# Moving the silu, product and split of an expert's hidden values behind TensorE's part of them, and parking the second embedding's products in DRAM

## The chip, the cores and the metric

One core of one Trainium2 chip runs the whole program. The metric is device time in microseconds (us), from one execution of the program, median of several; lower is better. The engines are TensorE (PE, with its weight loads shown apart as PEld), VectorE (DVE), ScalarE (ACT), GpSimd (POOL) and SyncE (SP), whose queue (SPq) issues nearly all the loads of weights.

## The reference

A trunk of two layers over 256 tokens of width 1024, all in float32. Nearly all of the change lies in the second layer's mixture of experts: each token goes to 2 of 8 experts, and each expert is a SwiGLU of width 3584. After it a per-layer embedding is added, which multiplies a product `p @ w_proj` (1024 columns for 256 tokens) by a gate.

```python
def swiglu_of_expert(xb, e):
    g, u = jnp.split(xb @ w_gate_up[e], 2, axis=-1)   # 1024 -> 2 x 3584
    return (jax.nn.silu(g) * u) @ w_down[e]           # 3584 -> 1024
...
h = h + moe_swiglu(rmsnorm(h, norm_ffn_g[i]), moe_router[j], moe_w_gate_up[j], moe_w_down[j])
h = h + per_layer_embed(h, p[i], norm_ple_g[i], ple_w_proj[i], ple_w_gate[i])
def per_layer_embed(h, p_i, g_norm, w_proj, w_gate):
    gate = jax.nn.sigmoid(rmsnorm(h, g_norm) @ w_gate)
    return (p_i @ w_proj) * gate
```

## The kernel before

Layer 0 and layer 1's mixers take about the first 520 us; layer 1's experts take most of the rest, to about 1450 us; the embedding's gate and the last norm follow.

**Weights.** An expert's weights come in tiles of 1 MB ("raw" tiles, `r_gu` for gate and up, `r_d` for down, `r_dl` for the last ones), loaded by SP into 11 buffers. Float32 products are made of two parts of the weights: `wsplit` writes for each half tile a high part `h` or `h_d` (a copy with rounding on ACT, line 145) and a low part `l` or `l_d` (raw minus high, on DVE, line 146). Both go through 4 buffers each.

**Experts.** The program goes through the experts 0 to 7 in order of their load, the most loaded first. Experts 0 to 3 ("large") have 128 slots and three products for each tile (high by high, low by high, high by low). Experts 4 to 7 ("few") have 64 slots; the high and low part of the tokens lie side by side in the 128 columns, so that two products do for each tile.

**Chunks.** The 3584 channels of an expert are cut into chunks of 1024, 1024, 1024 and 512. `gate_up(e, c)` multiplies a chunk's gate and up weights over 8 channel tiles k of the input, into banks `mg` and `mu`. Meanwhile the chunk before is finished: at the first row of tile k = 1 (`MID`), the function `mid()` calls `h_T`, which makes of the chunk before what `down` multiplies with the down weights. `down` then runs after the products of `gate_up`; `between` calls `activate`, which empties `mg` and `mu`, in the middle of it.

**Hidden values.** A block is 512 channels, so a chunk has two blocks, and the last has one. For a large expert `activate` makes silu and product (lines 1191 and 1192), and `h_T` transposes a block on PE (`mt`, line 1220) and splits it into `mhh` and `mhl`. For a few expert `activate` only copies gate and up out (`msg`, `msu`, line 1188), and `h_T` does for each block: 16 small products by `both` on PE that turn the block and add its two halves (`mt`, in one of 2 banks), the silu on ACT (`mgu`, line 1211), the product on DVE (`mgu`, line 1212), and the split, `mh` on ACT (line 197) and on DVE (line 198). These 16 products are called a turn below.

**Order.** Nothing of this is the final order: a scheduler puts the instructions of each engine in a fixed order by its own costs, and each engine then works its list from the top. An instruction that waits holds back all that stand behind it on that engine.

**The embedding's products.** The four tiles `pj` (128 by 512) of the second embedding are made early: `todo` holds those that are left for `mid()` of chunk 1 of expert 0 (`LATE`), and ACT copies them out (line 387). They stay in 4 of the 12 buffers of the tag `s2`, which also holds `msg`, `msu`, `mgu`, `mh`, `mhh` and `mhl`, until the end.

Of the kernel before, what the change touches and what calls it, by code (L numbers as in the profile page):

```python
# [8 lines left out]
F32 = mybir.dt.float32  # L9
F32R = mybir.dt.float32r  # L10
I32 = mybir.dt.int32
AF = mybir.ActivationFunctionType
ALU = mybir.AluOpType
AX = mybir.AxisListType
MUL, ADD, SUB, MAX = ALU.mult, ALU.add, ALU.subtract, ALU.max

P = 128
D = 1024
T = 256
NB = 2  # L20
# [4 lines left out]
NE = 8  # L25
# [58 lines left out]
def trunk_kernel(  # L84
# [6 lines left out]
    pe, act, dve, pool, sync = nc.tensor, nc.scalar, nc.vector, nc.gpsimd, nc.sync  # L91
# [5 lines left out]
    dr = ctx.enter_context(tc.tile_pool(name="dr", bufs=1, space=bass.MemoryType.DRAM))  # L97
# [5 lines left out]
    def s2(name, shape, dt=F32):  # L103
        return ar.tile(list(shape), dt, tag="s2", name=name, bufs=S2_BUFS)

    def py(name, shape=(P, 512)):
        return ps.tile(list(shape), F32, tag="y", name=name, bufs=2)

    def pt(name, shape=(P, 512)):
        return ps.tile(list(shape), F32, tag="t", name=name, bufs=2)  # L110
# [41 lines left out]
    def after(*names):  # L152

        stack = ExitStack()
        for n in names:
            stack.enter_context(tc.issue_after(last[n].ins))
        return stack
# [15 lines left out]
    def mm(o, a, b, start, stop, shared=False):  # L173
        last["mm"] = pe.matmul(o, a, b, start=start, stop=stop, skip_group_check=shared)  # L174
# [20 lines left out]
    def split(dst, src, scale=None):  # L195
        if scale is None:
            last["high"] = act.copy(dst[0], src)
            last["split"] = dve.tensor_tensor(dst[1], src, dst[0].bitcast(F32), SUB)
        else:
            last["high"] = act.activation(dst[0], src, AF.Copy, scale=scale)  # L200
            last["split"] = dve.scalar_tensor_tensor(dst[1], src, scale, dst[0].bitcast(F32), MUL, SUB)

    def sub2(pr, *idx):
        return pr[0][idx], pr[1][idx]
# [738 lines left out]
    def layer1_moe(pT):  # L943
# [110 lines left out]
        def few(e):  # L1054
            return e >= FEW
# [106 lines left out]
        def products(e, triples, start, stop):  # L1162


            if not few(e):
                return mm3s(triples, start, stop)
            for part in range(2):
                for o, a, b in triples:
                    mm(o, a, b[part], start and part == 0, stop and part == 1)

        def gate_up(e, c, mid):
            ns = CHUNKS[c][1] // 512
            banks = [[pa(f"m{nm}{e}{c}{i}") for i in range(ns)] for nm in "gu"]
            for k, j, wt in gate_up_weights(e, c):
                if (k, j) == (MID, 0):
                    mid()
                products(e, [(banks[j][i], tokens[e][k], sub2(wt, slice(None), slice(i * 512, i * 512 + 512))) for i in range(ns)],
                         k == 0, k == KT - 1)

            def activate():  # L1180

                res = []
                with after("wcopy", "wsplit"):
                    for i in range(ns):
                        if few(e):
                            res.append([s2(f"ms{nm}{e}{c}{i}", [P, 512]) for nm in "gu"])
                            for j in range(2):
                                act.copy(res[i][j], banks[j][i])
                            continue
                        sg = s2(f"msg{e}{c}{i}", [P, 512])  # L1190
                        act.activation(sg, banks[0][i], AF.Silu)
                        dve.tensor_tensor(sg, banks[1][i], sg, MUL)
                        res.append(sg)
                return res

            return activate

        def h_T(e, c, sgs):

            res = []  # L1200

            for i, sg in enumerate(sgs):
                if few(e):

                    q = pt(f"mt{e}{c}{i}", (P, 2, 4, P // 2))
                    for j in range(2):
                        for g in range(2):
                            for k in range(2):
                                mm(q[:, j, 2 * g + k, :], sg[j][:, 256 * g + k : 256 * g + 256 : 2], both, True, True)
                    t = s2(f"mgu{e}{c}{i}", [P, 4, P // 2])  # L1210
                    act.activation(t, q[:, 0], AF.Silu)
                    dve.tensor_tensor(t, q[:, 1], t, MUL)
                    hT = s2(f"mh{e}{c}{i}", [P, 4, 2, P // 2], F32R)
                    split((hT[:, :, 0], hT[:, :, 1]), t)
                    res += [hT[:, k].rearrange("q i s -> q (i s)") for k in range(4)]
                    continue
                q = pt(f"mt{e}{c}{i}", (P, 4, P))
                for g in range(2):
                    for k in range(2):
                        pe.transpose(q[:, 2 * g + k, :], sg[:, 256 * g + k : 256 * g + 256 : 2], ident)  # L1220
                hT = (s2(f"mhh{e}{c}{i}", [P, 4, P], F32R), s2(f"mhl{e}{c}{i}", [P, 4, P], F32R))
                split(hT, q)
                res += [sub2(hT, slice(None), k) for k in range(4)]
            return res

        def down(e, c, hT, yb, between):

            c0, n = CHUNKS[c]
            res = None
            for g in range(n // 256):  # L1230
                nm = f"d{e}_{c}_{g}"
                view = expert(moe_w_down, e)[c0 + g * 256 : c0 + g * 256 + 256].rearrange("(q k) c -> q k c", k=2)
                wt = wload(view, (2, D), nm, spare(nm))
                for i in range(2):
                    products(e, [(yb[half], hT[2 * g + i], sub2(wt[i], slice(None), HALF[half])) for half in range(2)],
                             c == g == i == 0, c == len(CHUNKS) - 1 and g == n // 256 - 1 and i == 1)
                if g == n // 512 - 1 and between:
                    res = between()
            return res

        def combine(e, yb, half):
            s = slice(half * 512, half * 512 + 512)
# [5 lines left out]
                mm(q, slots[e][:, b, :], yp[1], False, True)  # L1248
                dve.scalar_tensor_tensor(h[:, b, s], q, Gr[:, b, e : e + 1], h[:, b, s], MUL, ADD)

        yb, hT = {}, {}
        both = sm("both", (P, P // 2))
        dve.tensor_tensor(both, ident[:, : P // 2], ident[:, P // 2 :], ADD)

        def back(e, c, between=None):
            if c == 0:
                yb[e] = [py(f"y{e}{half}") for half in range(2)]
            if (e, c) == (NE - 1, len(CHUNKS) - 1):
                part = hT.pop((e, c))
                rows = expert(moe_w_down, e)[CHUNKS[c][0] :].rearrange("(g q k) c -> g q k c", k=2, q=P)  # L1260
                for half in range(2):
                    raw = wr.tile([P, 4, 512], F32, tag="raw", name=f"r_dl{half}", bufs=RAW_BUFS)
                    for g in range(2):
                        sync.dma_start(raw[:, 2 * g : 2 * g + 2], rows[g][:, :, HALF[half]])
                    wt = wsplit(raw, f"dl{half}")
                    for k in range(4):
                        products(e, [(yb[e][half], part[k], wt[k])], False, k == 3)
                    combine(e, yb[e], half)
                    last_norm[1](half)
                return  # L1270
            res = down(e, c, hT.pop((e, c)), yb[e], between)
            if c == len(CHUNKS) - 1:
                for half in range(2):
                    combine(e, yb[e], half)
            return res

        def more_slots(e, pos):

# [58 lines left out]

            return over > P, more

        prev = None  # L1340
        for e in range(NE):
            for c in range(len(CHUNKS)):
                if e % 2 == 1 and c == 2 and e <= FEW - 1:
                    spread_slots = gather(e // 2 + 1)
                if (e, c) == (FEW, 1):
                    spread_slots()

                def mid():
                    if prev:
                        hT[prev] = h_T(*prev, sg)  # L1350
                    if (e, c) == (0, LATE):
                        for bn in todo:
                            product(*bn, pt)
                            copy(*bn)

                activate = gate_up(e, c, mid)
                if prev:
                    sg = back(*prev, activate)
                else:
                    sg = activate()  # L1360
                    with after("wsplit"):
                        gates()
                prev = e, c
        mid()
        last_norm = halves_norm_T("ple1")
        back(*prev)

        return pj1, (last_norm[0], last_norm[2]()), overflow

# [79 lines left out]
RAW_BUFS = 11  # L1449
PAD = 8  # L1450
CONV_DVE = (31, 31, 5, 9)
MID = 1
FEW = 4
X_DVE = (3, 7)
PRODUCTS = (0, 2, 1, 0)
LATE = 1
# [36 lines left out]
```

## Time and profile before

| | |
|---|---|
| median of 3 runs | 1497.31 us (1495.36 to 1500.3) |
| the profiled execution | 1497.28 us |
| its span in the profile | 1495.5 us |
| mean granted TensorE clock | 0.995 of full speed |
| busy, share of the span | PE 97%, DVE 85%, ACT 72%, POOL 0% |
| moved by DMA | 438.26 MB |

The span is the time from the first to the last recorded instruction. Busy shares are averages over parts with different limits, so each part is read by itself: large experts until about 1010 us, few experts from about 1040 to 1446 us, then the tail.

### The profile page before, as it was taken

The numbers are of one execution on the slowest core, as the hardware profiler recorded it, in microseconds if no ns is written. First come the engines' busy times: TensorE is split into PE (matmuls) and PEld (weight loads), VectorE is DVE, ScalarE is ACT, GpSimd is POOL, SyncE is SP. The second block draws the span as 40 slices with busy tenths as digits, with TensorE's granted clock in tenths as the row PEclk, the third lists the DMA queues.
The fourth block names the chain that finished last, engine by engine and source line by source line (L and its number), as shares of the span: only waits on it lengthen the run. The fifth ranks groups of instructions, "written<-read, shape, count | busy, mean of one in ns | idle before, by whom it ended". The sixth has DMA issues, their size and how long they took to land.

```text
span 1495.5 us, 22012 instructions
## 1 busy us (share of the span) xinstructions
PE 1444.5 (97%) x7726; PEld 1194.7 (80%) x7726; DVE 1268.0 (85%) x1716; ACT 1076.1 (72%) x1441; POOL 4.9 (0%) x14
## 2 busy tenths in 40 slices
PE   7999999999999999999999999999999999999996
PEld 6999899988888878888888888886766666666665
DVE  6778655556698699999999989989999999999997
ACT  6545544446547678887887877779988988988975
POOL 0000000000000000000000000000000000000000
PEclk9999999999999999999999999999999999999998
DMA  9614656555452469898898998999999999999961
GB/s 350 241 43 131 216 177 196 172 195 185 147 203 106 149 248 354 327 410 333 322 376 336 392 347 341 359 363 389 377 409 414 390 413 410 388 413 408 394 254 44
DMA packets 136610, 438.26 MB, mean 293 GB/s; under 512 B 9067, under 2 KB 34188, under 8 KB 122412
## 3 DMA queue, kind: packets, MB, share of 16 engines
q1 hardware_dynamic: 132960, 433.19, 77.3%
q10 hardware_dynamic: 3148, 2.31, 0.5%
q0 software_dynamic: 384, 1.29, 0.4%
q8 instruction: 62, 1.02, 0.3%
q14 instruction: 56, 0.46, 0.1%
HBM read 434.92 MB, written 1.84 MB: 292 GB/s over the span
## 4 chain that ended last, share of the span: by engine, by line
PE 71%; DVE 18%; issue 4%; ACT 4%; DMA 3%; ACTq 0%; DVEq 0%; POOL 0%; POOLq 0%
PE y L174 14%; PE mg L174 11%; PE mu L174 11%; DVE l L146 11%; PE fu L174 4%; PE fg L174 4%; PE fd L174 4%; PE wo L174 3%; PE pg L174 3%; PE mt L174 2%; DMA r_gu<-in_moe_w_gate_up_dram 2%; DVE l_d L146 2%; PE p L174 1%; PE mt L1220 1%; PE in_og L174 1%
## 5 line engine op out<-in xcount | busy, mean ns | idle before, releaser
L146 DVE TENSOR_TENSOR l<-r_gu,h 128x1024 fp32r<-128x1024 f32 x448 | 526.3, 1218 | 18.1 <-ACT h L145 6.3
L145 ACT CAST h<-r_gu 128x1024 fp32r<-128x1024 f32 x448 | 456.6, 1052 | 60.2 <-PE mu L174 22.4
L146 DVE TENSOR_TENSOR l_d<-r_d,h_d 128x1024 fp32r<-128x1024 f32 x220 | 258.6, 1219 | 16.7 <-ACT h_d L145 10.4
L145 ACT CAST h_d<-r_d 128x1024 fp32r<-128x1024 f32 x220 | 226.8, 1054 | 24.7 <-PE mu L174 10.3
L146 DVE TENSOR_TENSOR l_gu<-r_gu,h_gu 128x1024 fp32r<-128x1024 f32 x44 | 53.8, 1224 | 47.7 <-ACT h_gu L145 47.7
L145 ACT CAST h_gu<-r_gu 128x1024 fp32r<-128x1024 f32 x44 | 46.0, 1048 | 64.2 <-PE fu L174 49.0
L174 PE MATMUL y<-l_d,mh 128*128 128x512 f32 x216 | 75.3, 430 | 3.7 <-DVE l_d L146 3.7
L174 PE MATMUL y<-l_d,mhh 128*128 128x512 f32 x224 | 69.8, 393 | 0.1
L174 PE MATMUL y<-h_d,mh 128*128 128x512 f32 x216 | 69.2, 402 | 0.3
L174 PE MATMUL y<-h_d,mhh 128*128 128x512 f32 x224 | 69.4, 391 | 0.0
L174 PE MATMUL y<-h_d,mhl 128*128 128x512 f32 x224 | 69.1, 390 | 0.0
L174 PEld LDWEIGHTS y<-l_d,mh 128*128 128x128 f32 x216 | 34.4, 188 | 27.4 <-DVE l_d L146 25.1
L146 DVE TENSOR_TENSOR l_fd<-r_fd,h_fd 128x1024 fp32r<-128x1024 f32 x22 | 26.9, 1224 | 27.3 <-ACT h_fd L145 26.3
L174 PE MATMUL fg<-x_ffn0h,h_gu 128*128 128x256 f32 x176 | 49.9, 283 | 0.0
L174 PE MATMUL fu<-x_ffn0h,h_gu 128*128 128x256 f32 x176 | 49.9, 283 | 0.0
L174 PE MATMUL fg<-x_ffn0h,l_gu 128*128 128x256 f32 x176 | 49.9, 283 | 0.0
L174 PE MATMUL fu<-x_ffn0l,h_gu 128*128 128x256 f32 x176 | 49.8, 283 | 0.0
L174 PE MATMUL fu<-x_ffn0h,l_gu 128*128 128x256 f32 x176 | 49.8, 283 | 0.0
L174 PE MATMUL fg<-x_ffn0l,h_gu 128*128 128x256 f32 x176 | 49.8, 283 | 0.0
L174 PEld LDWEIGHTS y<-h_d,mhl 128*128 128x128 f32 x224 | 42.1, 188 | 8.9
L174 PEld LDWEIGHTS y<-l_d,mhh 128*128 128x128 f32 x224 | 41.5, 188 | 9.5 <-DVE l_d L146 1.4
L174 PEld LDWEIGHTS y<-h_d,mhh 128*128 128x128 f32 x224 | 41.8, 188 | 8.9 <-ACT h_d L145 0.4
(719 smaller groups left out, 3673.6 us busy)
## 6 DMA issues: line engine op xcount, KB each, us to landing
r_gu<-in_moe_w_gate_up_dram SPq DMA_DIRECT2D x192, 1024.0 KB, 7.7
r_d<-in_moe_w_down_dram SPq DMA_DIRECT2D x110, 1024.0 KB, 7.7
r_gu<-in_moe_w_gate_up_dram SPq DMA_DIRECT2D x64, 512.0 KB, 6.4
r_gu<-in_ffn_w_gate_up_dram SPq DMA_DIRECT2D x44, 512.0 KB, 4.4
r_fd<-in_ffn_w_down_dram SPq DMA_DIRECT2D x11, 1024.0 KB, 4.9
r_wo<-in_ev_w_out_dram SPq DMA_DIRECT2D x4, 1024.0 KB, 12.8
r_pg<-in_ple_w_gate_dram SPq DMA_DIRECT2D x4, 1024.0 KB, 7.0
r_wo<-in_od_w_out_dram SPq DMA_DIRECT2D x4, 1024.0 KB, 5.0
```

Source lines behind the costliest of these rows:

```text
L145: last["wcopy"] = act.copy(wh, raw[:, i : i + step])
L146: last["wsplit"] = dve.tensor_tensor(wl, raw[:, i : i + step], wh.bitcast(F32), SUB)
L174: last["mm"] = pe.matmul(o, a, b, start=start, stop=stop, skip_group_check=shared)
L1220: pe.transpose(q[:, 2 * g + k, :], sg[:, 256 * g + k : 256 * g + 256 : 2], ident)
```

## The change

The part of `h_T` that belongs to a few expert is taken apart. Where all of it was called at k = 1, four functions are now called at the channel tiles `MIDS` = (1, 3, 2, 5) of the next `gate_up`: `turn` (PE) at k = 1, `turned` (silu on ACT and product on DVE, of both blocks, into one tile `mgu`) at k = 3, `across` (the large experts' transposes) at k = 2 and the split `h_T` at k = 5. The loop over `back` goes by blocks instead of chunks. The four `pj` tiles are written to a DRAM tile `pj1d` by ACT's queue, right after they are made, and loaded again by SP's queue ahead of the last block; in between their `s2` buffers serve the hidden values.

```diff
-        def gate_up(e, c, mid):
+        def gate_up(e, c, at):
 ...
-                if (k, j) == (MID, 0):
-                    mid()
+                if j == 0 and k in at:
+                    at[k]()
...
-        def h_T(e, c, sgs):
+        def turn(e, c):
             res = []
-            for i, sg in enumerate(sgs):
-                if few(e):
-                    q = pt(f"mt{e}{c}{i}", (P, 2, 4, P // 2))
-                    for j in range(2):
-                        for g in range(2):
-                            for k in range(2):
-                                mm(q[:, j, 2 * g + k, :], sg[j][:, 256 * g + k : 256 * g + 256 : 2], both, True, True)
-                    t = s2(f"mgu{e}{c}{i}", [P, 4, P // 2])
-                    act.activation(t, q[:, 0], AF.Silu)
-                    dve.tensor_tensor(t, q[:, 1], t, MUL)
-                    hT = s2(f"mh{e}{c}{i}", [P, 4, 2, P // 2], F32R)
-                    split((hT[:, :, 0], hT[:, :, 1]), t)
-                    res += [hT[:, k].rearrange("q i s -> q (i s)") for k in range(4)]
-                    continue
...
+            for i, sg in enumerate(hidden[e, c]):
+                q = pt(f"mt{e}{c}{i}", (P, 2, 4, P // 2))
+                for j in range(2):
+                    for g in range(2):
+                        for k in range(2):
+                            mm(q[:, j, 2 * g + k, :], sg[j][:, 256 * g + k : 256 * g + 256 : 2], both, True, True)
+                res.append(q)
             return res
...
+        def turned(e, c, banks):
+            t = s2(f"mgu{e}{c}", [P, len(banks), 4, P // 2])
+            for i, q in enumerate(banks):
+                act.activation(t[:, i], q[:, 0], AF.Silu)
+                dve.tensor_tensor(t[:, i], q[:, 1], t[:, i], MUL)
+            hidden[e, c] = t
+
+        def across(e, c, i):
+            if few(e):
+                return None
+            q = pt(f"mt{e}{c}{i}", (P, 4, P))
+            for g in range(2):
+                for k in range(2):
+                    pe.transpose(q[:, 2 * g + k, :], hidden[e, c][i][:, 256 * g + k : 256 * g + 256 : 2], ident)
+            return q
+
+        def h_T(e, c, i, q):
+            if few(e):
+                hT = s2(f"mh{e}{c}{i}", [P, 4, 2, P // 2], F32R)
+                split((hT[:, :, 0], hT[:, :, 1]), hidden[e, c][:, i])
+                return [hT[:, k].rearrange("q i s -> q (i s)") for k in range(4)]
...
+        stored = dr.tile([P, NB, 2, 512], F32, name="pj1d")
...
+            def turn_fresh():
+                if fresh and few(fresh[0]):
+                    banks["fresh"] = turn(*fresh)
+                if now == (0, LATE):
+                    for bn in todo:
+                        product(*bn, pt)
+                        copy(*bn)
+                    for b, i in BLOCKS:
+                        act.dma_start(stored[:, b, i], pj1[b][i])
+
+            def fresh_turned():
+                if "fresh" in banks:
+                    turned(*fresh, banks["fresh"])
...
+                activate = gate_up(*now, dict(zip(MIDS, (turn_fresh, fresh_turned, blocks_across, blocks_split))))
...
         last_norm = halves_norm_T("ple1")
-        back(*prev)
+        for b, i in BLOCKS:
+            pj1[b][i] = s2(f"pj1{b}{i}", [P, 512])
+            sync.dma_start(pj1[b][i], stored[:, b, i])
+        hT[downs[0]] = h_T(*downs[0], across(*downs[0]))
+        back(*downs[0])
...
-MID = 1
+MIDS = (1, 3, 2, 5)
```

What the scheduler makes of it is read from the built programs. The first place is on ACT, where expert 4's chunk 1 is turned while the down weights of its chunk 0 are split (names `h_d_x_2` and `h_d_x_3` are the high parts of that chunk's third and fourth raw tile, whose numbers go from 0). Before:

```order
L145 CAST h_d_0_2_0_11315<-r_d_0_2_11313 128x1024
L145 CAST h_d_0_2_1_11319<-r_d_0_2_11313 128x1024
L1211 ACTIVATE mgu_11390<-mt_11381 128x256
L145 CAST h_d_0_3_0_11333<-r_d_0_3_11331 128x1024
L145 CAST h_d_0_3_1_11337<-r_d_0_3_11331 128x1024
L197 CAST mh_11393<-mgu_11390 128x4x64
L1211 ACTIVATE mgu_11405<-mt_11396 128x256
```

and after:

```order
L145 CAST h_d_0_2_0_11316<-r_d_0_2_11314 128x1024
L145 CAST h_d_0_2_1_11320<-r_d_0_2_11314 128x1024
L1215 ACTIVATE mgu_11436<-mt_11382 128x256
L1215 ACTIVATE mgu_11436<-mt_11391 128x256
L145 CAST h_d_0_3_0_11334<-r_d_0_3_11332 128x1024
L145 CAST h_d_0_3_1_11338<-r_d_0_3_11332 128x1024
L197 CAST mh_11477<-mgu_11436 128x4x64
```

The silu of the second block has moved from behind the fourth raw tile's high parts to ahead of them. The same two lists stand at 8 places, the turns of chunks 1 and 2 of the experts 4 to 7. On DVE at the same place, before:

```order
L146 TENSOR_TENSOR l_d_0_2_1_11320<-r_d_0_2_11313,h_d_0_2_1_11319 128x1024
L1212 TENSOR_TENSOR mgu_11390<-mt_11381,mgu_11390 128x256
L146 TENSOR_TENSOR l_d_0_3_0_11334<-r_d_0_3_11331,h_d_0_3_0_11333 128x1024
L146 TENSOR_TENSOR l_d_0_3_1_11338<-r_d_0_3_11331,h_d_0_3_1_11337 128x1024
L198 TENSOR_TENSOR mh_11393<-mgu_11390,mh_11393 128x4x64
```

and after:

```order
L146 TENSOR_TENSOR l_d_0_2_1_11321<-r_d_0_2_11314,h_d_0_2_1_11320 128x1024
L1216 TENSOR_TENSOR mgu_11436<-mt_11382,mgu_11436 128x256
L146 TENSOR_TENSOR l_d_0_3_0_11335<-r_d_0_3_11332,h_d_0_3_0_11334 128x1024
L146 TENSOR_TENSOR l_d_0_3_1_11339<-r_d_0_3_11332,h_d_0_3_1_11338 128x1024
L1216 TENSOR_TENSOR mgu_11436<-mt_11391,mgu_11436 128x256
```

Here the first product and the low parts behind it stand where they stood; the second product comes ahead of the split. PE's list is the same in both at these places. The third place is ACT at the turn of chunk 0, in the middle of `gate_up` of chunk 1 (experts 5 to 7 alike; expert 4 has its own order). Before:

```order
L145 CAST h_1_3_1_11183<-r_gu_1_3_11177 128x1024
L1211 ACTIVATE mgu_11130<-mt_11121 128x256
L145 CAST h_1_4_0_11197<-r_gu_1_4_11195 128x1024
L197 CAST mh_11133<-mgu_11130 128x4x64
L1211 ACTIVATE mgu_11145<-mt_11136 128x256
L145 CAST h_1_4_1_11201<-r_gu_1_4_11195 128x1024
```

and after:

```order
L145 CAST h_1_3_1_11173<-r_gu_1_3_11167 128x1024
L1215 ACTIVATE mgu_11177<-mt_11123 128x256
L1215 ACTIVATE mgu_11177<-mt_11132 128x256
L145 CAST h_1_4_0_11192<-r_gu_1_4_11190 128x1024
L145 CAST h_1_4_1_11196<-r_gu_1_4_11190 128x1024
L197 CAST mh_11218<-mgu_11177 128x4x64
```

Both silus now stand ahead of `h_1_4_0`. On DVE the two products here stand behind `l_1_3_0` and `l_1_3_1`, ahead of `l_1_4_0`. The single-block turns of chunk 3 stand as before.

## Rows read from the trace of the kernel before

**Rows 1.** The page's first part: span, and busy time of each engine.

```profile
span 1495.5 us, 22012 instructions
PE 1444.5 (97%) x7726; PEld 1194.7 (80%) x7726; DVE 1268.0 (85%) x1716; ACT 1076.1 (72%) x1441; POOL 4.9 (0%) x14
```

**Rows 2.** Windows, large then few: busy us, engine by engine, PEclk, DMA share, GB/s.

```profile
560.00:1010.00 450.00, 449.85 (x2058) 373.20 (x2057) 416.05 (x407) 353.85 (x384) 0.00 (x0) 1.00 0.94 355
1040.00:1446.00 406.00, 388.23 (x1730) 277.61 (x1729) 389.31 (x389) 353.76 (x430) 0.00 (x0) 1.00 1.01 400
```

**Rows 3.** DVE's groups, 1040 to 1446: busy us, mean ns, idle before, releaser.

```profile
L146 DVE TENSOR_TENSOR l<-r_gu,h 128x1024 fp32r<-128x1024 f32 x206 | 238.0, 1216 | 0.1
L146 DVE TENSOR_TENSOR l_d<-r_d,h_d 128x1024 fp32r<-128x1024 f32 x106 | 122.8, 1217 | 8.2 <-ACT h_d L145 8.2
L1212 DVE TENSOR_TENSOR mgu<-mt,mgu 128x256 f32<-128x256 f32 x27 | 11.4, 421 | 7.8 <-ACT mgu L1211 7.7
```

**Rows 4.** The waits of all engines, 1040 to 1446: us in total, times, longest.

```profile
PEld mu L174 <- DVE l L146: 42.8, 74, 0.8
ACT mgu L1211 <- PE mt L174: 32.7, 18, 3.4
ACT h L145 <- DMA r_gu<-in_moe_w_gate_up_dram: 0.9, 2, 0.6
```

**Rows 5.** The waits of SP's queue, 1050 to 1440, the largest.

```profile
SPq L766 <- DVE l L146: 94.1, 52, 4.2
```

**Rows 6.** Timeline of expert 5's chunk 1 turn: start, us, [idle before <-releaser].

```profile
1175.62 1.11 PE L174 MATMUL mt<-both,msu 128*128 128x64 f32 x8
1176.77 0.38 ACT L1211 ACTIVATE mgu<-mt 128x256 f32<-128x256 f32 x1 [2.01 <-PE mt L174]
1177.05 1.98 ACT L145 CAST h_d<-r_d 128x1024 fp32r<-128x1024 f32 x2
1177.18 0.42 DVE L1212 TENSOR_TENSOR mgu<-mt,mgu 128x256 f32<-128x256 f32 x1 [0.59 <-ACT mgu L1211]
1177.96 1.11 PE L174 MATMUL mt<-both,msu 128*128 128x64 f32 x8
1178.12 2.36 DVE L146 TENSOR_TENSOR l_d<-r_d,h_d 128x1024 fp32r<-128x1024 f32 x2 [0.51 <-ACT h_d L145]
```

**Rows 7.** Timeline: the first (expert 4) and the last (expert 7) such turn pairs.

```profile
1066.50 1.11 PE L174 MATMUL mt<-both,msu 128*128 128x64 f32 x8
1068.83 1.11 PE L174 MATMUL mt<-both,msu 128*128 128x64 f32 x8
...
1423.71 1.11 PE L174 MATMUL mt<-both,msu 128*128 128x64 f32 x8
1426.05 1.11 PE L174 MATMUL mt<-both,msu 128*128 128x64 f32 x8
```

**Rows 8.** Timeline of expert 5's chunk 0 turn, in the middle of chunk 1.

```profile
1157.34 2.35 DVE L146 TENSOR_TENSOR l<-r_gu,h 128x1024 fp32r<-128x1024 f32 x2
1158.47 0.39 ACT L1211 ACTIVATE mgu<-mt 128x256 f32<-128x256 f32 x1 [0.26 <-PE mt L174]
1158.75 1.04 ACT L145 CAST h<-r_gu 128x1024 fp32r<-128x1024 f32 x1
1160.28 1.22 DVE L146 TENSOR_TENSOR l<-r_gu,h 128x1024 fp32r<-128x1024 f32 x1
```

**Rows 9.** Timeline of PE at expert 0's first products.

```profile
531.11 0.50 PE L174 MATMUL mg<-h,xe0h 128*128 128x512 f32 x1 [0.75 <-ACT pj L387]
```

**Rows 10.** The last raw tiles, by tile and by timeline: issue, landing, first use.

```profile
L145 ACT CAST h_dl<-r_dl x4: 1046/1047/1052, 1448.6 to 1451.4; 128x1024 fp32r<-128x1024 f32 x4
DMA to landing us min/median/max: 8.4/9.0/9.6
...
1422.45 3.56 SPq L1264 DMA_DIRECT2D r_dl<-in_moe_w_down_dram  x4
```

**Rows 11.** A DMA issue on ACT's queue: ns min/median/max, first and last start.

```profile
L798 ACTq DMA_DIRECT2D bd<-fbs x4: 326/344/448, 394.4 to 409.2; - x4
```

More of the change, by code (lines that the diff above doesn't have):

```diff
@@ L1196, in gate_up @@
             return activate
-        def h_T(e, c, sgs):
+        def turn(e, c):
             res = []
-            for i, sg in enumerate(sgs):
-                if few(e):
-                    q = pt(f"mt{e}{c}{i}", (P, 2, 4, P // 2))
-                    for j in range(2):
-                        for g in range(2):
-                            for k in range(2):
-                                mm(q[:, j, 2 * g + k, :], sg[j][:, 256 * g + k : 256 * g + 256 : 2], both, True, True)
-                    t = s2(f"mgu{e}{c}{i}", [P, 4, P // 2])
-                    act.activation(t, q[:, 0], AF.Silu)
-                    dve.tensor_tensor(t, q[:, 1], t, MUL)
-                    hT = s2(f"mh{e}{c}{i}", [P, 4, 2, P // 2], F32R)
-                    split((hT[:, :, 0], hT[:, :, 1]), t)
-                    res += [hT[:, k].rearrange("q i s -> q (i s)") for k in range(4)]
-                    continue
[L1217 to L1223, printed above, removed]
-            return res
@@ L1226, in down @@
-        def down(e, c, hT, yb, between):
+            for i, sg in enumerate(hidden[e, c]):
[5 more added lines that the diff above has]
+                res.append(q)
+            return res
+        def turned(e, c, banks):
[4 more added lines that the diff above has]
+            hidden[e, c] = t
@@ new lines, in across @@
+        def across(e, c, i):
[11 more added lines that the diff above has]
+                return [hT[:, k].rearrange("q i s -> q (i s)") for k in range(4)]
+            hT = (s2(f"mhh{e}{c}{i}", [P, 4, P], F32R), s2(f"mhl{e}{c}{i}", [P, 4, P], F32R))
+            split(hT, q)
+            return [sub2(hT, slice(None), k) for k in range(4)]
@@ L1228, in down @@
+        def down(e, c, i, hT, yb, between):
             c0, n = CHUNKS[c]
-            res = None
-            for g in range(n // 256):
+            for g in range(2 * i, 2 * i + 2):
                 nm = f"d{e}_{c}_{g}"
@@ L1233, in down @@
                 wt = wload(view, (2, D), nm, spare(nm))
[L1234 to L1239, printed above, removed]
+                for k in range(2):
+                    products(e, [(yb[half], hT[2 * (g % 2) + k], sub2(wt[k], slice(None), HALF[half])) for half in range(2)],
+                             c == g == k == 0, c == len(CHUNKS) - 1 and g == n // 256 - 1 and k == 1)
+                if g == 2 * i and between:
+                    between()
         def combine(e, yb, half):
@@ L1249, in combine, with back @@
                 dve.scalar_tensor_tensor(h[:, b, s], q, Gr[:, b, e : e + 1], h[:, b, s], MUL, ADD)
-        yb, hT = {}, {}
+        yb, hT, hidden = {}, {}, {}
         both = sm("both", (P, P // 2))
         dve.tensor_tensor(both, ident[:, : P // 2], ident[:, P // 2 :], ADD)
-        def back(e, c, between=None):
-            if c == 0:
+        def back(e, c, i, between=None):
+            if c == i == 0:
                 yb[e] = [py(f"y{e}{half}") for half in range(2)]
+            part = hT.pop((e, c, i))
             if (e, c) == (NE - 1, len(CHUNKS) - 1):
-                part = hT.pop((e, c))
                 rows = expert(moe_w_down, e)[CHUNKS[c][0] :].rearrange("(g q k) c -> g q k c", k=2, q=P)
@@ L1270, in back @@
                 return
-            res = down(e, c, hT.pop((e, c)), yb[e], between)
+            down(e, c, i, part, yb[e], between)
             if c == len(CHUNKS) - 1:
@@ L1274, in back @@
                     combine(e, yb[e], half)
-            return res
         def more_slots(e, pos):
@@ L1338, in overflow @@
             return over > P, more
[L1340 to L1363, printed above, removed]
@@ L1364, in layer1_moe, with blocks_across, blocks_split, between @@
-        mid()
-        last_norm = halves_norm_T("ple1")
-        back(*prev)
+        gates_up = [(e, c) for e in ORDER for c in range(len(CHUNKS))]
+        downs = [(e, c, n) for e in ORDER for c in range(len(CHUNKS)) for n in range(CHUNKS[c][1] // 512)]
+        stored = dr.tile([P, NB, 2, 512], F32, name="pj1d")
+        fresh = None
+        while gates_up or len(downs) > 1:
+            now = gates_up.pop(0) if gates_up else None
+            step = NE * len(CHUNKS) - len(gates_up) - 1 if now else None
+            n = next((i for i, d in enumerate(downs) if d[:2] not in hidden), len(downs))
+            n = min(1 if now and step < RAMP else 2, n, sum(d[0] == downs[0][0] for d in downs))
+            blocks, downs = downs[:n], downs[n:]
+            if step == QUAD:
+                spread_slots = gather(2)
+            if step == SLOTS:
+                spread_slots()
+            if step == PAIR:
+                gather(1)
+            banks = {}
+            def turn_fresh():
[10 more added lines that the diff above has]
+                    turned(*fresh, banks["fresh"])
+            def blocks_across():
+                for d in blocks:
+                    banks[d] = across(*d)
+            def blocks_split():
+                for d in blocks:
+                    hT[d] = h_T(*d, banks[d])
+            if now:
+                activate = gate_up(*now, dict(zip(MIDS, (turn_fresh, fresh_turned, blocks_across, blocks_split))))
+                def between(now=now, activate=activate):
+                    hidden[now] = activate()
+            else:
+                for f in (turn_fresh, fresh_turned, blocks_across, blocks_split):
+                    f()
+                between = None
+            for i, d in enumerate(blocks):
+                back(*d, between if len(blocks) == 1 else None)
+                if i == 0 and len(blocks) == 2 and between:
+                    between()
+            if not blocks:
+                between()
+            if step == 0:
+                with after("wsplit"):
+                    gates()
+            fresh = now
@@ L1368, in layer1_moe @@
+        if fresh:
+            turned(*fresh, turn(*fresh))
+        last_norm = halves_norm_T("ple1")
+        for b, i in BLOCKS:
[3 more added lines that the diff above has]
+        back(*downs[0])
         return pj1, (last_norm[0], last_norm[2]()), overflow
@@ L1451 @@
 CONV_DVE = (31, 31, 5, 9)
-MID = 1
+MIDS = (1, 3, 2, 5)
+RAMP = 0
+ORDER = (0, 1, 2, 3, 4, 5, 6, 7)
 FEW = 4
+QUAD, SLOTS, PAIR = 14, 17, 6
 X_DVE = (3, 7)
```

## The prediction

> **What bounds the kernel now.** I began with the page's first part [rows 1]: TensorE is busy for 97% of the span, and no other engine comes near. Taken alone that says that only TensorE's work counts. The windows view says otherwise [rows 2]. In the large experts' 450 us TensorE is busy for 449.85 us, at the full granted clock (1.00, the level of 2.4 GHz): it is the bound. In the few experts' 406 us TensorE is busy for 388.2 us and VectorE for 389.3 us. The two are equally busy, so the shares can't say which of them sets the pace; what each waits for must.
>
> VectorE's groups of this stretch answer it [rows 3]. VectorE sits idle for 406 − 389.3 = 16.7 us, and 16.0 of these stand before two groups: 8.2 us before the low parts `l_d`, for ACT's `h_d`, and 7.8 us before the products `mgu`, for ACT's silu. Before the 206 low parts `l` it waits 0.1 us in all. So VectorE never waits for a weight or for a free buffer, only for ACT beside the turns. The view of all waits shows the other side [rows 4]: TensorE's loads wait 42.8 us for VectorE's `l` in one group alone (these waits partly lie under running products), while ACT waits 32.7 us for the turns `mt` and 0.9 us for a weight that hasn't landed. SP's queue waits for VectorE to free raw buffers, 94.1 us in its largest group [rows 5]: the loads run ahead until all buffers are full. So in the few stage the chain is: VectorE works through the tiles, TensorE and SP follow it, and nothing behind it can make up for time that VectorE loses. A microsecond of added VectorE idleness there is a microsecond at the end.
>
> **What the change does on that path.** In the order the decisive pair is at the turns of chunks 1 and 2 of the experts 4 to 7. Before, ACT did the silu of the first block, then the two high parts `h_d_x_3`, and only then the silu of the second block. Now the second silu stands ahead of the high parts. It reads the second bank `mt`, so it waits for the second turn on TensorE, and the high parts are queued behind it; VectorE's next low part `l_d_x_3_0` waits for them.
>
> The price is read from the timeline [rows 6]. The first turn's last products run from 1175.62 for 1.11 us and end at 1176.73; ACT's silu starts at 1176.77, having waited 2.01 us; the high parts start 0.28 us later (1177.05), VectorE's low part 1.07 us after that (1178.12), with 0.51 us of idleness. The second turn ends at 1177.96 + 1.11 = 1179.07. With the new order the silu of the first block ends as it did; the second can't start before 1179.07 + 0.04 = 1179.11, the high parts start 0.28 later, at 1179.39, and the low part 1.07 later, at 1180.46. That is 1180.46 − 1178.12 = **2.34 us** later, exactly the distance between the ends of the two turns. TensorE works through that distance without a pause and its list there is unchanged, so the distance should be the same after. It is 2.33 us at the first pair (1066.50 to 1068.83) and 2.34 us at the last (1423.71 to 1426.05) [rows 7], and between 2.33 and 2.34 at all 8. I take 8 × 2.34 = **18.7 us**. What was to cover it would be VectorE work that could go before the low part; the order has only the first product there, in both versions, so there is no cover. Nor does the shorter list behind it (the split and the second product come later by one or two places) give time back: these instructions are all still made, of the same shapes.
>
> **The other parts.**
> - *Turns of chunk 0*, 4 places. The second silu is again ahead of a high part, `h_1_4_0`. Here VectorE has cover. The silu runs where it ran, at 1158.47, and the high part behind it at 1158.75, for 1.04 us, to 1159.79 [rows 8]. VectorE's two low parts (2.35 us, which began at 1157.34, one product's step of 0.34 us after the silu's product at 1157.00) move up to 1157.00 and end at 1159.35; with two products, 0.42 us each by [rows 3] and some 0.34 apart, it comes to `l_1_4_0` at about 1160.05, 0.25 us after the high part is ready. I take 0; if the cover is gone, the cost is at most the high part's 1.04 us less what is left of VectorE's work, some 0.5 us a place, so 0 to 2.0 us. Nothing can be gained, since VectorE's wait there is nil.
> - *Large experts*. Transposes come a tile later, and the high and low parts of their hidden values too. TensorE has 450 − 449.85 = 0.15 us of idleness there in all [rows 2], so nothing is to be gained, and the count of its instructions is unchanged: 0. A loss would need TensorE to wait for a split that comes later; the splits are used only in `down`, a full tile's products and more after k = 5. I take 0, and 0 to 1 us for the range.
> - *Early products of the embedding.* Some of the `pj` products move into the start of expert 0, where TensorE sat idle for 0.75 us until ACT had copied one out [rows 9]. Between 0 and −0.75; since products stand in that very gap now, −0.7.
> - *Writing `pj1d`.* Four DMA issues on ACT. The nearest row is an issue on ACT's queue of 326 to 448 ns [rows 11], so some 1.4 us of ACT's time while the large experts run, where ACT is busy 353.9 of 450 us [rows 2]: hidden under TensorE, 0. Without that cover it is 1.4 us.
> - *Reading it back.* Four loads stand in SP's queue behind the first `r_dl` load and ahead of the other three and of the gate's weights. They fill `s2` buffers that `msg` and `msu` of expert 7's chunk 2 leave, so SP waits for the second turn there, which ends at 1427.16 [rows 7]. The `r_dl` issues ran from 1422.45 for 3.56 us; now the last three follow the turn and four issues of some 0.5 us, to about 1431. They land at most 9.6 us later, at 1440.6, and ACT first reads them at 1448.6 [rows 10]: 8 us of cover remain, so 0. Were it gone, the price is the shift itself, some 5 to 6 us.
> - *Tail.* ACT's and VectorE's last few instructions change places: −1 to +1, I take 0.
>
> **Sum.** 1497.28 (the profiled execution, its span plus 1.8 us around it; the median of the runs, 1497.31, is the same) + 18.7 − 0.7 = **1515.3 us**.
>
> **A rule weighed.** VectorE's idleness comes at the same two spots of every turn. The Trainium skill, Perfetto Trace Analysis, Optimization Strategy, says that consistent bubbles on the engine that should be saturated can mean that SBUF or PSUM has too little room for the next tile. By that rule the four `s2` buffers that this change frees would remove all 16.7 us of idleness, for 1480.6 us. The trace disagrees as far as it shows: the releasers named [rows 3, 6] are ACT's results, and behind them the turn.
>
> **Rivals.**
> - *Faster.* TensorE could reach the turns earlier against ACT. Where both turns were done before ACT came to the silus, neither would wait, and the 0.59 + 0.51 = 1.10 us of VectorE's wait at each of 8 places [rows 6] would go: −8.8 us, 1488.5 us. It decides from the point where the second turn ends before ACT is free, and ACT now waits 2.01 us for the first: the turns would have to come 2.01 + 2.34 = 4.35 us earlier. TensorE's order there is unchanged and it works right behind VectorE, so this is not likely: 0.04. The case in which freed buffers remove the idleness gets 0.02.
> - *No change.* The transfers could be what sets the pace: the DMA engines' share is 1.01 at 400 GB/s in the few stage [rows 2]. Then VectorE would make up each delay out of its wait for data, and the time stays at 1497 us. Against it stands SP's 94.1 us of waiting for VectorE [rows 5], and ACT's 0.9 us for a raw tile [rows 4]: 0.06. (The Trainium skill, DMA: Bandwidth & Descriptors, Specifications, gives a fabric ceiling of 435 GB/s; the trace's 400 GB/s is below it.)
> - *Partly absorbed.* TensorE's and ACT's backlog shifts so that half the delays are met by shorter waits elsewhere, 1502 to 1510 us: 0.08.
> - *Slower still.* The loads of `pj` delay `r_dl` or the gate's weights by the 5 to 6 us above, or the chunk 0 turns add 2 us: 1517 to 1523 us, 0.08.
>
> **How the numbers follow.** The forecast of 1515.3 us has a chance of 0.72; its own range, from the bounds (−0.05 to +1.4, +2, +1, ±1), is 1513 to 1519. The range of 8 in 10 takes in the upper part of the partly absorbed case and the lower part of the slower one: 1508 to 1520 us. A change of 0.3% (4.5 us, 1492.8 to 1501.8 us) is about what a measurement of this kernel can tell from none. Faster holds the two cases of 0.04 and 0.02, together 0.06; the same 0.06; slower the other three, 0.88.
>
> **What would show it.** In the profile after: at the 8 places ACT's second silu right behind the first, with a wait of about 1.95 us for `mt`; VectorE's wait before `l_d` there of 2.85 us (0.51 + 2.34) where it was 0.51; VectorE's idleness before `l_d` in the few stage of about 27 us where it was 8.2, its busy time unchanged, and the stage longer by some 19 us; the large stage as long as before with TensorE full; no wait of ACT for `r_dl` or a gate weight. I would be wrong if the second turn ended sooner behind the first than 2.3 us, if VectorE's added waits were matched by shorter ones at other instructions, or if the last loads came late.

## The result, and the profile after

The changed kernel takes 1514.58 us (median of 4 runs, 1513.64 to 1516.05), the kernel before 1497.3 us: a ratio of 1.0114, interval 1.0095 to 1.0134, so it is slower by some 17.3 us. The forecast was 1515.3 us. The profiled execution took 1515.27 us, with a span of 1513.4 us, 17.9 us longer than before [rows 1].

The page's first part of the changed kernel:

```profile
span 1513.4 us, 22024 instructions
PE 1454.0 (96%) x7726; PEld 1193.1 (79%) x7726; DVE 1267.8 (84%) x1716; ACT 1074.9 (71%) x1441; POOL 4.9 (0%) x14
```

VectorE has the same 1716 instructions and is busy for 1267.8 us, where it was 1268.0. No engine but TensorE has more busy time, and the page warns that a busy PE is modelled from matmul ends; TensorE's count is unchanged. So it is idleness that was added, and the question is where.

The windows of the changed kernel, large experts, then few experts (columns as in [rows 2]; the second window is 18 us longer than there, since the stage is):

```profile
560.00:1010.00 450.00, 449.92 (x2060) 373.53 (x2059) 416.88 (x409) 353.88 (x386) 0.00 (x0) 1.00 0.94 357
1040.00:1464.00 424.00, 395.49 (x1724) 274.35 (x1723) 388.28 (x388) 351.72 (x428) 0.00 (x0) 1.00 1.00 384
```

TensorE fills the first window in both kernels, so a window of fixed length can't show whether the large stage has become shorter. Two points of the program can: TensorE's first product of expert 0 and its last products of `y` for a large expert, first before, then after:

```profile
528.37 0.40 PE L174 MATMUL mg<-h,xe0h 128*128 128x512 f32 x1
1037.22 0.62 PE L174 MATMUL y<-l_d,mhh 128*128 128x512 f32 x2
...
528.90 0.40 PE L174 MATMUL mg<-h,xe0h 128*128 128x512 f32 x1
1036.09 0.62 PE L174 MATMUL y<-l_d,mhh 128*128 128x512 f32 x2
```

From the start of the one to the end of the other it is 509.5 us before and 507.8 us after: the large stage is 1.65 us shorter. The few stage can be measured in the same way, from there to VectorE's first low part of the last raw tiles:

```profile
1450.06 4.62 DVE L146 TENSOR_TENSOR l_dl<-r_dl,h_dl 128x1024 fp32r<-128x1024 f32 x4
...
1468.24 3.49 DVE L146 TENSOR_TENSOR l_dl<-r_dl,h_dl 128x1024 fp32r<-128x1024 f32 x3
```

It takes 412.2 us before and 431.5 us after, 19.3 us more. In the window of the few stage VectorE is idle for 424 − 388.3 = 35.7 us, where it was 16.7: 19.0 us more. The DMA engines moved 384 GB/s where they had moved 400, at a full DMA share in both: the loads slowed down with VectorE.

VectorE's groups of that window say ahead of what (busy us, mean ns, idle before, releaser):

```profile
L146 DVE TENSOR_TENSOR l<-r_gu,h 128x1024 fp32r<-128x1024 f32 x205 | 237.0, 1219 | 0.3
L146 DVE TENSOR_TENSOR l_d<-r_d,h_d 128x1024 fp32r<-128x1024 f32 x106 | 122.9, 1220 | 26.9 <-ACT h_d L145 24.0 <-DMA r_gu<-in_moe_w_gate_up_dram 2.9
...
L1216 DVE TENSOR_TENSOR mgu<-mt,mgu 128x256 f32<-128x256 f32 x27 | 11.1, 422 | 8.2 <-ACT mgu L1215 8.2
```

Against [rows 3], `l_d` went from 8.2 to 26.9 us of idleness before it, 18.7 us more; `l` and `mgu` stayed within 0.4 us. (The 2.9 us put down to a load of `r_gu` are one wait out of the same series: a low part `l_d` doesn't read that tile, and its size is that of the others.)

The timeline of the changed kernel at expert 5's chunk 1 turn, the place of [rows 6]:

```profile
1179.54 1.11 PE L174 MATMUL mt<-both,msu 128*128 128x64 f32 x8
1180.69 0.38 ACT L1215 ACTIVATE mgu<-mt 128x256 f32<-128x256 f32 x1 [1.99 <-PE mt L174]
1181.10 0.42 DVE L1216 TENSOR_TENSOR mgu<-mt,mgu 128x256 f32<-128x256 f32 x1 [0.56 <-ACT mgu L1215]
1181.88 1.11 PE L174 MATMUL mt<-both,msu 128*128 128x64 f32 x8
1183.02 0.39 ACT L1215 ACTIVATE mgu<-mt 128x256 f32<-128x256 f32 x1 [1.95 <-PE mt L174]
1183.30 1.99 ACT L145 CAST h_d<-r_d 128x1024 fp32r<-128x1024 f32 x2
1184.38 2.36 DVE L146 TENSOR_TENSOR l_d<-r_d,h_d 128x1024 fp32r<-128x1024 f32 x2 [2.85 <-ACT h_d L145]
1184.40 0.30 PEld L174 LDWEIGHTS y<-h_d,mh 128*128 128x128 f32 x2 [0.40 <-ACT h_d L145]
1185.66 0.74 PE L174 MATMUL y<-l_d,mh 128*128 128x512 f32 x2 [0.52 <-DVE l_d L146]
```

ACT's second silu waits 1.95 us for the second turn, the two high parts start right behind it, and VectorE waits 2.85 us for them, where it waited 0.51. From the start of the first turn's last products to the start of the low part it is 1184.38 − 1179.54 = 4.84 us, where it was 1178.12 − 1175.62 = 2.50: 2.34 us. TensorE runs out of `h_d` and then of `l_d`. The other turns of chunks 1 and 2 read alike: in all 8 of them the second silu waits 1.95 or 1.96 us for `mt`, and VectorE 2.85 us for `h_d`.

The waits of all engines in that window, against [rows 4]:

```profile
ACT mgu L1215 <- PE mt L174: 51.9, 26, 3.1
```

It was 32.7 us in 18 waits. The 8 new ones are the second silus, 8 x 1.95 = 15.6 us; most of the rest of the 19.2 us is at chunk 0's turns, where the second silu of the experts 5 to 7 now waits 1.50 us in place of 0.26 and VectorE hardly notices (0.06 us before a low part that follows, at each of the three).

The tiles of `r_dl` and `pj` at the end, against [rows 10] (ns min/median/max, first and last start in us):

```profile
L1275 SPq DMA_DIRECT2D r_dl<-in_moe_w_down_dram x4: 543/548/554, 1438.3 to 1445.1; - x4
L145 ACT CAST h_dl<-r_dl x4: 1042/1047/1050, 1466.4 to 1472.1; 128x1024 fp32r<-128x1024 f32 x4
DMA to landing us min/median/max: 7.4/7.6/8.2
...
L1377 ACTq DMA_DIRECT2D pj1d<-pj x4: 326/326/332, 536.0 to 556.4; - x4
L1415 SPq DMA_DIRECT2D pj<-pj1d x4: 319/322/343, 1439.8 to 1443.1; - x4
```

The last `r_dl` is issued at 1445.1 and lands by 1453.3 or so, 13 us ahead of the first high part that is made of any of the four.

### The profile page after: what moved, and what is told of

Its sections match the earlier page's. It is cut to its first block, busy times and chain, and to the rows that moved or that the text cites. A ratio compares the mean times of both kernels' runs of the same rounds, so it can differ in the third digit from the quotient of the medians.

```text
span 1513.4 us, 22024 instructions
## 1 busy us (share of the span) xinstructions
PE 1454.0 (96%) x7726; PEld 1193.1 (79%) x7726; DVE 1267.8 (84%) x1716; ACT 1074.9 (71%) x1441; POOL 4.9 (0%) x14
## 3 DMA queue, kind: packets, MB, share of 16 engines
q8 instruction: 62, 1.02, 0.3%
## 4 chain that ended last, share of the span: by engine, by line
PE 69%; DVE 17%; DMA 5%; ACT 4%; issue 4%; ACTq 0%; DVEq 0%; POOL 0%; POOLq 0%
PE y L174 13%; PE mu L174 11%; PE mg L174 11%; DVE l L146 10%; PE fu L174 4%; PE fg L174 4%; PE fd L174 4%; PE wo L174 3%; DMA r_gu<-in_moe_w_gate_up_dram 3%; PE pg L174 3%; DVE l_d L146 3%; PE mt L174 2%; DMA r_d<-in_moe_w_down_dram 2%; PE p L174 1%; PE mt L1226 1%
## 5 line engine op out<-in xcount | busy, mean ns | idle before, releaser
L1215 ACT ACTIVATE mgu<-mt 128x256 f32<-128x256 f32 x28 | 10.8, 384 | 55.0 <-PE mt L174 55.0
L146 DVE TENSOR_TENSOR l_fd<-r_fd,h_fd 128x1024 fp32r<-128x1024 f32 x22 | 26.9, 1225 | 27.3 <-ACT h_fd L145 26.3
L174 PEld LDWEIGHTS y<-h_d,mh 128*128 128x128 f32 x216 | 38.5, 188 | 13.5 <-ACT h_d L145 6.3
```

The costliest lines, as they stand in the source:

```text
L146: last["wsplit"] = dve.tensor_tensor(wl, raw[:, i : i + step], wh.bitcast(F32), SUB)
L1215: act.activation(t[:, i], q[:, 0], AF.Silu)
```

## The experiments

All times are medians, with the ratio to the kernel before and its interval. The first four runs shared their runs of the kernel before (1497.03 us), as did the next two (1497.57 us) and the last two (1496.93 us).

**1. The second silu put back, all else as changed.** `last["down"]` notes the last high part of a `down`; `after` holds an instruction behind a noted one.

```diff
 # down()
                 wt = wload(view, (2, D), nm, spare(nm))
+                last["down"], last["down_l"] = last["wcopy"], last["wsplit"]
 # turned()
             for i, q in enumerate(banks):
-                act.activation(t[:, i], q[:, 0], AF.Silu)
+                with after("down") if i and c else ExitStack():
+                    act.activation(t[:, i], q[:, 0], AF.Silu)
                 dve.tensor_tensor(t[:, i], q[:, 1], t[:, i], MUL)
```

> The changed kernel with one thing put back: at the turns of chunks 1 and 2 the second block's silu stands behind the high parts h_d_x_3 again. Theory (the silu's wait for the second turn ahead of h_d_x_3 is the whole loss): the 8 waits of 2.34 us go, 1514.6 - 18.7 = 1496 us, ratio to the kernel before about 0.999; VectorE's idleness before l_d in the few stage back from 26.9 to about 8 us. Rival 1 (the DRAM store and reload of the embedding's products, or the later splits, cost the time): stays at about 1514. Rival 2 (half from each): about 1505.

Measured: 1496.67 us, ratio 0.9995 (0.9986 to 1.0005). VectorE's group in the few stage of this run (1040 to 1445):

```profile
L146 DVE TENSOR_TENSOR l_d<-r_d,h_d 128x1024 fp32r<-128x1024 f32 x106 | 122.8, 1217 | 8.2 <-ACT h_d L145 7.7 <-DMA r_gu<-in_moe_w_gate_up_dram 0.5
```

The idleness is back at 8.2 us, and the whole loss is gone, while the DRAM tile, the transposes a tile later and the split at k = 5 are all still there. Between the two points named above the few stage takes 412.9 us in this run, 18.6 us less than in the changed kernel. The places of 8 silus are the cause. What is left of the change is too small for the times, but the points show it: the large stage is 1.6 us shorter here too, and the few stage 0.7 us longer than before.

**2. The DRAM tile taken out, the pairs left in.** The four `pj` stay in their `s2` buffers.

```diff
-                    for b, i in BLOCKS:
-                        act.dma_start(stored[:, b, i], pj1[b][i])
...
-        for b, i in BLOCKS:
-            pj1[b][i] = s2(f"pj1{b}{i}", [P, 512])
-            sync.dma_start(pj1[b][i], stored[:, b, i])
```

> The changed kernel without the DRAM tile: the pj tiles stay in their four s2 buffers; the silus still come in pairs. Theory: the pairs are untouched, so 1514 to 1516 us, VectorE's idleness before l_d about 27 us. Rival 1 (store and reload cost the time): back to 1497 to 1500. Rival 3 (the freed s2 buffers hide part of the pairs' cost, so that without them it is dearer): over 1518.

Measured: 1515.05 us, ratio 1.0123 (1.0106 to 1.0139), with 26.9 us of idleness before `l_d`, the same as with the tile. Its two stages, between the same points, are within 0.1 us of the changed kernel's. Storing the products neither costs nor gives time, and neither do the four freed buffers.

**3. The pairs alone, in the kernel before.**

```diff
 # h_T() of the kernel before
+            if few(e) and c:
+                ts, qs = [], []
+                for i, sg in enumerate(sgs):
+                    q = pt(f"mt{e}{c}{i}", (P, 2, 4, P // 2))
 ...
+                    qs.append(q)
+                for i, q in enumerate(qs):
+                    t = s2(f"mgu{e}{c}{i}", [P, 4, P // 2])
+                    act.activation(t, q[:, 0], AF.Silu)
+                    dve.tensor_tensor(t, q[:, 1], t, MUL)
+                    ts.append(t)
+                for i, t in enumerate(ts):
+                    hT = s2(f"mh{e}{c}{i}", [P, 4, 2, P // 2], F32R)
+                    split((hT[:, :, 0], hT[:, :, 1]), t)
```

> The kernel before with one part of the change alone: at the turns of chunks 1 and 2 of the few experts both turns, then both silus and products, then both splits, all at channel tile 1; nothing else moved, pj kept in SBUF. Theory: the second silu stands ahead of h_d_x_3 at the same 8 places, so 1497.3 + 18.7 = 1516 us, 0.7 to 0.9 us above the changed kernel, which fills TensorE's gap at expert 0's start. Rival 1: no DRAM tile, so 1497. Rival 4 (the loss needs the split to come four tiles later than the turn as well): 1497 to 1505.

Measured: 1516.59 us, ratio 1.0127 (1.0111 to 1.0144). The timeline of this run at expert 5's chunk 1 turn:

```profile
1185.40 0.39 ACT L1213 ACTIVATE mgu<-mt 128x256 f32<-128x256 f32 x1 [2.01 <-PE mt L174]
1185.68 1.99 ACT L145 CAST h_d<-r_d 128x1024 fp32r<-128x1024 f32 x2
1186.75 2.36 DVE L146 TENSOR_TENSOR l_d<-r_d,h_d 128x1024 fp32r<-128x1024 f32 x2 [2.91 <-ACT h_d L145]
```

It is enough to write both silus behind both turns, all at k = 1: the same wait appears at the same place, and the same loss. The time is 2.0 us above the changed kernel's, where 0.7 to 0.9 were expected: the large stage takes 509.5 us, as before, and so 1.6 us more than in the changed kernel. That the silu and the split come two or four tiles later in the code is not what costs.

**4. Half of the places.** As experiment 1, with `if i and c == 1` in place of `if i and c`.

> The changed kernel with the second silu put back at the turns of chunk 1 alone, 4 places of 8. Theory: each place counts for itself, so 4 x 2.34 = 9.4 us are given back, 1505 us. Rival 5 (the stalls of one expert are one queue's backlog, so that undoing half of them gives back all or nothing): 1496 or 1514.

Measured: 1505.27 us, ratio 1.0054 (1.0037 to 1.0071). Four places give back 1514.58 − 1505.27 = 9.3 us, 2.33 us each. VectorE's group in the few stage (1040 to 1455):

```profile
L146 DVE TENSOR_TENSOR l_d<-r_d,h_d 128x1024 fp32r<-128x1024 f32 x106 | 122.8, 1218 | 17.6 <-ACT h_d L145 16.0 <-DMA r_gu<-in_moe_w_gate_up_dram 1.5
```

17.6 lies half way between 8.2 and 26.9. Each place counts for itself.

**5 and 6. Both silus behind the high parts.** If VectorE's waits for ACT go one to one to the end, the 16.7 us that the kernel before has of them are to be had too. On the kernel before (experiment 5):

```diff
 # h_T() of the kernel before, with last["down"] noted as in experiment 1
-                    act.activation(t, q[:, 0], AF.Silu)
-                    dve.tensor_tensor(t, q[:, 1], t, MUL)
+                    with after("down") if c else ExitStack():
+                        act.activation(t, q[:, 0], AF.Silu)
+                    with after("down_l") if c else ExitStack():
+                        dve.tensor_tensor(t, q[:, 1], t, MUL)
```

On the changed kernel (experiment 6) the same in `turned`, with the second block held behind the first high and low parts of the next `gate_up`.

> The kernel before, with each few expert's silus at the turns of chunks 1 to 3 held behind the high parts h_d_x_3, and the first products behind their low parts; the second silu then falls behind the next gate_up's first high parts. Theory (VectorE's wait for ACT beside the turns goes one to one to the end): the 8 waits of 0.59 + 0.51 us and the 4 of chunk 3 (about 1.5 us each) go, 8.8 to 15 us faster, 1482 to 1488 us; VectorE's idleness in the few stage from 16.7 to 2 to 8 us. Rival 6 (TensorE, busy 388 us there, is as much the bound as VectorE, so that it makes the waits its own): 1493 to 1497 us, with VectorE's idleness now before l, for free buffers.

> The changed kernel with its silus and products held in the same way, the second silu behind the next gate_up's first high parts. Theory: 1514.6 - 18.7 - (8.8 to 15), 1480.5 to 1487 us, 0.7 to 0.9 us below the same edit on the kernel before. Rival 6: 1493 to 1496 us.

Measured: 1489.19 us (1487.69 to 1489.28), ratio 0.9941 (0.9924 to 0.9957), and 1489.81 us, ratio 0.9948 (0.9931 to 0.9964). Both beat the kernel before, but by 1 to 3 us less than the least that was expected, and the second is not ahead of the first: its large stage is 1.8 us shorter than that of experiment 5, but its few stage is 0.7 us longer, and the rest, from the first `l_dl` to the end, 1.1 us longer (46.5 against 45.4). VectorE's groups and one wait of ACT in the few stage of experiment 5 (1040 to 1438):

```profile
L146 DVE TENSOR_TENSOR l<-r_gu,h 128x1024 fp32r<-128x1024 f32 x206 | 239.8, 1219 | 7.3 <-ACT mgu L1212 3.2 <-ACT h L145 2.1 <-issue 1.9
L146 DVE TENSOR_TENSOR l_d<-r_d,h_d 128x1024 fp32r<-128x1024 f32 x105 | 120.7, 1219 | 2.6 <-ACT h_d L145 2.6
L1214 DVE TENSOR_TENSOR mgu<-mt,mgu 128x256 f32<-128x256 f32 x27 | 11.3, 420 | 0.1
```

```profile
ACT h L145 <- PE y L174: 15.9, 16, 1.3
```

The waits before `l_d` and `mgu` are gone (16.0 us to 2.7), but 7.3 us stand before `l` now, where there were 0.1. (The page puts 3.2 us of them down to `mgu`, which a low part doesn't read; what it needs of ACT is `h`.) ACT's high parts now wait 15.9 us for TensorE's products `y`, a group that has no line among the waits of the kernel before. The reading taken from this, that a high part waits until TensorE has left one of the four buffers, is what the next two runs test. Idleness before `l` for want of buffers is the sign that rival 6 named; the time lies between the two forecasts.

**7 and 8. One buffer more for high and low parts.** Five instead of four, for one raw buffer of eleven, on the kernel of experiment 5 and, as a control, on the kernel before.

```diff
-RAW_BUFS = 11
+RAW_BUFS = 10
-SPL_BUFS = 4
+SPL_BUFS = 5
```

> The kernel before with both silus held behind the high parts, and 5 buffers instead of 4 for the high and the low parts each, paid for by one raw buffer (10 instead of 11). In the run with 4 buffers ACT waited 15.9 us in the few stage for TensorE to leave a high part's buffer, and VectorE 7.3 us before l. Theory: that wait is the next one in line, so about 5 to 7 us more, 1482 to 1485 us. Rival 6 (TensorE itself is the bound by now): 1488 to 1490. Rival 7 (one raw buffer fewer starves the loads): over 1492.

> The kernel before with the same buffers (5, 5 and 10) and nothing else. Theory: VectorE's 16.7 us of idleness there are waits for ACT behind the turns and not for room, so 1496 to 1498 us. Rival (the repeated gaps come from too few buffers): 1481 to 1490.

Measured: 1480.99 us (1479.45 to 1482.98), ratio 0.989 (0.9874 to 0.9907), 1 us under the expected 1482 to 1485, and 1497.39 us, ratio 1.0001 (0.9991 to 1.001). VectorE's groups in the few stage, first with both edits, then of the control:

```profile
L146 DVE TENSOR_TENSOR l<-r_gu,h 128x1024 fp32r<-128x1024 f32 x207 | 240.0, 1216 | 0.0
L146 DVE TENSOR_TENSOR l_d<-r_d,h_d 128x1024 fp32r<-128x1024 f32 x105 | 120.7, 1217 | 2.6 <-ACT h_d L145 2.6
```

```profile
L146 DVE TENSOR_TENSOR l_d<-r_d,h_d 128x1024 fp32r<-128x1024 f32 x106 | 122.8, 1218 | 8.2 <-ACT h_d L145 8.2
```

The same buffer is worth some 8 us (1489.19 − 1480.99) where the silus are out of the way and nothing where they are not. The window of the kernel with both edits, from 1040 to 1430:

```profile
1040.00:1430.00 390.00, 377.70 (x1723) 279.59 (x1721) 387.28 (x390) 351.28 (x432) 0.00 (x0) 1.00 1.02 408
```

VectorE is idle for 2.7 us of 390. This is the fastest version of the study, 15.9 us ahead of the kernel before.

## Why the prediction was right

**The bound and the chain.** The prediction said that in the few stage VectorE sets the pace, although TensorE is as busy, and that its added idleness goes to the end one to one. Shown: 18.7 us more before `l_d` and 19.3 us more of few stage, of which 18.6 go when the 8 silus are put back; the span grew by 17.9 because the large stage lost 1.65. By the times 4 places give 9.3 us, 8 give 17.9 (1514.58 − 1496.67). And in the other direction, taking waits away made the kernel faster.

**The price of a place.** 2.34 us by the distance of two turns; measured 2.34 us on the timeline and 2.85 against 0.51 us of wait, as forecast. 8 × 2.34 = 18.7 us is what the group shows. The two signs named for it, the second silu's wait of about 1.95 us and about 27 us before `l_d`, came out at 1.95 and 26.9.

**The terms taken as nothing.** Chunk 0's turns were taken as 0, with 0 to 2.0 us allowed; they cost about 0.5. At expert 4 VectorE waits 0.47 us for the silu's result where it waited 0.13, and at the experts 5 to 7 the cover of the next low part holds, with 0.12 us to spare and not 0.25, but a later one waits 0.06 us. That is most of the 0.7 us by which the few stage of experiment 1 is longer than before. The four stores take ACT 326 ns each, within the row used. The loads of `pj` did hold `r_dl` back: its last issue came at 1445.1, the first high part 21 us later, so there was cover. Experiment 2 shows both together as nothing.

**The gain at the start of expert 0.** −0.7 us was taken, and this is the term that was mis-sized: the large stage is 1.65 us shorter. The gap of [rows 9] is gone, filled by products of `pj` (at 530.73). A second gap, which the prediction didn't name, stood at the start of expert 0's second chunk; two more of these products moved ahead of it, and it shrank from 0.98 to 0.52 us. Before, then after:

```profile
552.84 0.50 PE L174 MATMUL mg<-h,xe0h 128*128 128x512 f32 x1 [0.98 <-ACT msg L1191]
...
553.54 0.50 PE L174 MATMUL mg<-h,xe0h 128*128 128x512 f32 x1 [0.52 <-ACT msg L1192]
```

The two gaps make 1.2 of the 1.65 us; where the rest comes from stays open. The size is no chance of one profile: the stage takes 509.45 to 509.53 us in the kernel before and in experiments 3 and 5, and 507.77 to 507.86 in the changed kernel and in experiments 1, 2, 4 and 6, which leave its large stage as it is.

**Luck in the sum.** The forecast of 1515.3 us meets the profiled execution, 1515.27, in part because two small errors work against each other: 1 us too little gain in the large stage, and 0.7 us that the few stage lost and the sum did not have. The 18.7 us is not luck. The inner range of 1513 to 1519 us doesn't follow from the bounds named with it, which add up to some 1514.3 to 1520.7; the measured time lies in both.

**The rivals.** *Transfers set the pace* fell: the loads gave 16 GB/s less when VectorE slowed down (384 against 400), and 408 GB/s in experiment 7, at a DMA share of 1.00 and 1.02, so they follow, and the share that the rival rested on doesn't tell. *Earlier turns* fell by the timeline, where the first silu still waits 1.99 us; the time of 1488.5 us that the rival gave is about what experiments 5 and 6 reach (1489.2 and 1489.8 us) by taking the silus out of ACT's way instead. That is a coincidence: there some 13 us of waits went, not 8.8, and some 7 us came before `l`. *Freed buffers* fell with experiments 1, 2 and 8: experiment 1 has the four `s2` buffers free and still 8.2 us before `l_d`, and neither they nor a fifth split buffer moves the kernel by itself. *Partly absorbed* fell with 18.6 us for 8 places, *slower still* with loads that came in time and chunk 0 turns that cost 0.5 us. The rule of the Trainium skill (Perfetto Trace Analysis, Optimization Strategy) that repeated bubbles can mean too little room doesn't hold for the gaps of the kernel before, and does for those of experiment 5, which a fifth buffer took away. That the 1480.6 us of the rule's case is about what both edits reach (1480.99) is again a coincidence: other buffers, and only after the silus were moved.

## What to carry to other kernels

An instruction that waits costs what stands behind it on its engine. Before two like instructions are put side by side, see whether the second one's input comes later than the first's, and what is queued behind it: here a silu of 0.38 us that waited 1.95 us held up the high parts on which the pacing engine waits, and 8 of these made 1.2% of the kernel. Where two engines are equally busy, what each is idle for tells which one sets the pace. Whether a stage has become shorter is read between two points of the program and not from a window of fixed length. And a buffer more is worth trying again after a wait has been removed: here it gave nothing before and 8 us after.

## What was not expected of the hardware

Nothing in these runs is a behaviour of the chip that the prediction had otherwise. The repetition was closer than expected: the second silu's wait was between 1.95 and 1.96 us at all 8 places, and the distance of two turns 2.33 to 2.34 us at each. That experiment 5 came out at 1489 and not between 1482 and 1488 us was a limit of the program, the four buffers, as experiment 7 shows; experiment 6 was not run with a fifth.
